# Level 1 of a gated linear attention without a matmul group of its own

## The chip, the cores and the metric

The kernel runs on one core of a Trainium2 chip. The time is that of one execution on the device, in microseconds, from the first to the last instruction with what the device adds around it. Several runs are taken and their median is given.

## The reference

The program is a two-layer block. Each layer mixes three branches (retention with 4 heads, HGRN2 with 8 heads, differential attention with 8 heads) and has a convolutional feed-forward part. There are 16 meta tokens and 256 others, 272 in all, and the width is 1024. The change is in HGRN2 alone, which for one head of 128 features computes, in chunks of 128 tokens,

```python
def step(state, xs):
    qc, kc, vc, lfc = xs
    cb = jnp.cumsum(lfc, axis=1)                  # log of the forget gates, summed
    rel = cb[:, :, None] - cb[:, None, :]
    dec = jnp.where(causal, jnp.exp(jnp.where(causal, rel, 0.0)), 0.0)
    a = jnp.einsum('bqhd,bkhd,bqkhd->bhqk', qc, kc, dec)
    o = jnp.einsum('bhqk,bkhe->bqhe', a, vc) + jnp.einsum('bqhd,bhde->bqhe', qc * jnp.exp(cb), state)
    ...
```

The weight of key k for query q is thus a sum over the features of q times k times the product of the gates of the tokens k+1 to q, and each feature has gates of its own. For k = q there is no gate: the weight is the plain product of q and k.

## The kernel before

**The main stream.** All projections are matmuls of 128x128 weight tiles with 272 (in the second layer partly 258) columns of activations. Each is done three times, with high and low halves of weights and activations (`whi`, `wlo`, `xh`, `xl`; the lines L890 to L892), into tiles named `main`. Weights come by DMA in chunks of eight tiles (`wraw`); ScalarE rounds them to `whi`, and VectorE subtracts to get `wlo`. This stream runs from the beginning to the end, and everything else on TensorE is put between its matmuls.

**The planner.** Every step is recorded as an operation with an engine, a cost and a due time. A list scheduler (`_Plan.order`) then writes an order for every engine, and each engine works its list off in that order. The cost of a group of small matmuls is `0.02 * calls + 0.3`. So a change of one part can move other steps of the same stretch.

**HGRN2 (`hg_heads`).** It is called twice per layer, for the first and the second four heads. The weights within a chunk are built by levels of 64, 32, 16, 8, 4, 2 and 1 tokens: at level s, the tokens are taken in pairs of blocks of s, and the queries of the right block meet the keys of the left one. Queries are multiplied by the gates of their block up to themselves, and keys by the gates behind them; `total` holds the product of gates of each block, and `double` joins two blocks: it multiplies the keys of the left one by the right one's total, and the totals in pairs. The names in the profile are `hq` (queries), `hf` (keys), `he` (gates, the first `total`) and `tot` (later totals).

A group of matmuls for a level is made by `blocks` (L1075): for each head, 32 keys at a time are the stationary side, 128 features deep and 32 columns wide, so that four quarters of the array, each with its 32 columns, write four ranges of 32 partitions of one PSUM bank (`lev`). `quarters` lists the 32 calls of four heads, two chunks and four quarters. Level 4 goes with level 2, and level 16 with level 8: `quads` lists for four blocks of s tokens the queries in six versions (raw, or multiplied ahead), kept in `extra`; a call has 64 columns at level 2 and 48 at level 8. Masked copies (`copy_predicated` with the masks in `lev`) then pick the valid weights into `near`, a tile of 32x32 weights for each quarter, chunk and head. Levels 32 and 64 are made together in a far group of 40 calls (L1075 too), and copied with `near` into `at`, the weights of the four heads.

Before the change, level 1 has a group of its own:

```python
tt(right(q, 1), right(q, 1), right(total, 1), MUL)      # odd queries times their own gate
...
if s == 1:
    wide = pl[:, :256].rearrange("p (g t) -> p g t", g=8)
    quarters(wide, q, lambda hd, c, t: q[:, hd, tokens(c, t)])
    dve.copy_predicated(near, lev[:, 112:144].unsqueeze(1).to_broadcast([P, 8, 32]), wide)
```

Its 32 calls have 32 queries each. From its result the weights of even keys for themselves and for the odd query behind them are taken. The odd queries' own weights come with level 2, from raw odd queries that are part of its list. Afterwards all queries are multiplied by the first gate of their pair, and `double(1, T)` does the keys and totals.

The last 16 of the 272 tokens (the tail) have small matmuls of their own (`pm`, with copies in `kt` and `qt`) for the levels up to 8. For the levels above, the far group has four calls of 16 columns per head with the tail's queries (`late`), multiplied ahead by the totals of one to three blocks of 32 (`last_q`). At the end, the tail's queries are multiplied once more, and `px` takes all keys of the first chunk against the queries of the second chunk and the tail. `hg_outputs` (`ho`, `ht`) multiplies the weights by the values. GpSimd zeroes `at`, `am` and `near` at the start of `hg_heads`. Retention's first steps (`s`, `tw`, `ro`) follow on the second four heads.

Of the kernel before, what the change touches and what calls it, by code (L numbers as in the profile page):

```python
# [14 lines left out]
AF = mybir.ActivationFunctionType  # L15
# [4 lines left out]
P = 128  # L20
# [211 lines left out]
def _constants():  # L232
# [52 lines left out]
    block = [quads(2), quads(8), even(32, 32)]  # L285
    lev[:, :144] = np.tile(np.concatenate(block, axis=1), (4, 1))

# [346 lines left out]
def _trace(ctx, tc, plan, a, depth, probe):  # L634
# [330 lines left out]
    for li in range(depth):  # L965
# [72 lines left out]
        def hg_heads(b):  # L1038
# [30 lines left out]

            def blocks(calls, out, *moving):  # L1070


                def run():
                    for o, keys, x in calls:
                        nc.tensor.matmul(o, keys, x, start=True, stop=True)  # L1075

                plan.add("pe", run, 0.02 * len(calls) + 0.3, [out], [k, *moving])

            def quarters(out, moving, x):

                return blocks([(out[32 * t : 32 * t + 32, 2 * hd + c], k[:, hd, c * P + 32 * t : c * P + 32 * t + 32], x(hd, c, t))
                               for hd in hs for c in range(2) for t in range(4)], out, moving)

# [7 lines left out]


            act.activation(qt2[:, :, 8:], right(q[:, :, tail], 1)[:, :, :, 0], AF.Copy)
            act.activation(quads(2)[:, :, : 2 * P // 8, 12:], q[:, :, : 2 * P].rearrange("p h (n k two) -> p h n k two", k=4, two=2)[:, :, :, :, 1], AF.Copy)
            tt(right(q, 1), right(q, 1), right(total, 1), MUL)
            room, at0 = slot("tot"), 0
            for i, s in reversed(list(enumerate(LEVELS))):
# [4 lines left out]
                if s in (4, 16, 64):  # L1102
                    continue
                pl = bank("lev")
                tokens = lambda c, t: slice(c * P + 32 * t, c * P + 32 * t + 32)
                end = 2 * P if s > 8 else T
                if s == 1:
                    wide = pl[:, :256].rearrange("p (g t) -> p g t", g=8)
                    quarters(wide, q, lambda hd, c, t: q[:, hd, tokens(c, t)])
                    dve.copy_predicated(near, lev[:, 112:144].unsqueeze(1).to_broadcast([P, 8, 32]), wide)  # L1110
                elif s in (2, 8):
                    x = quads(s)
# [10 lines left out]
                    wide = pl[:, : 8 * each * width]  # L1123
                    quarters(wide.rearrange("p (g t) -> p g t", g=8), extra,
                             lambda hd, c, t: x[:, hd, (4 * c + t) * each : (4 * c + t + 1) * each, :].rearrange("p n x -> p (n x)"))
# [9 lines left out]
                    if s == 2:  # L1135
                        dve.copy_predicated(to.rearrange("p g n (k two) -> p g n k two", two=2)[:, :, :, :, 1], mask[:, :, :, 12:], wide[:, :, :, 12:])
                elif s == 32:
                    for t in range(4):
                        here = slice(32 * t, 32 * t + 32)
                        act.activation(at[here, :, : 2 * P].rearrange("p h (c t) -> p h c t", c=2)[:, :, :, here],  # L1140
                                       near[here].rearrange("p (h c) t -> p h c t", c=2), AF.Copy)


                    far_q = extra[:, : 8 * 96].rearrange("p (h n x) -> p h n x", h=4, n=2)
                    last_q = extra[:, 8 * 96 : 8 * 96 + 12 * TAIL].rearrange("p (n h t) -> p n h t", n=3, h=4)
                    qs = q[:, :, : 2 * P].rearrange("p h (n t) -> p h n t", n=2)
                    by = lambda c, m: total[:, :, :8].rearrange("p h (n c) -> p h n c", c=4)[:, :, :, c : c + 1].to_broadcast([P, 4, 2, m])
                    act.activation(far_q[:, :, :, :32], qs[:, :, :, 64:96], AF.Copy)
                    act.activation(far_q[:, :, :, 64:], qs[:, :, :, 96:], AF.Copy)
# [18 lines left out]
                    blocks(calls, far, q, far_q, last_q)  # L1168
                    for n in range(2):
                        for t, cols, x in ((0, slice(0, 96), 3 * n), (1, slice(0, 64), 1 + n), (2, slice(64, 96), 1 + n)):  # L1170
                            to = at[lanes[t], :, n * P + 32 * t + 32 : n * P + P]
                            if t == x:
                                dve.tensor_copy(to, far[lanes[x], :, cols])
                            else:
                                act.activation(to, far[lanes[x], :, cols], AF.Copy)
                    act.activation(at[:, :, tail], far[:, :, 96:], AF.Copy)
# [35 lines left out]
                if s == 1:  # L1212
                    qr = q.rearrange("p h (n two) -> p h n two", two=2)
                    tt(qr, qr, first.to_broadcast([P, 4, n, 2]), MUL)
                elif s in (2, 8):
# [6 lines left out]
                else:  # L1222

                    qr = q[:, :, P + 32 : 2 * P]
                    tt(qr, qr, total[:, :, 4:5].to_broadcast([P, 4, 96]), MUL)
                if s == 2:
                    total = parts
                else:
                    double(s, end, P if s == 32 else None)
# [442 lines left out]
```

## Time and profile before

| | us |
|---|---|
| runs before | 1318.12 median (1317.83 to 1318.2, 3 runs) |
| the profiled execution | 1318.41 |
| its span, first to last instruction | 1316.6 |
| TensorE busy in the span | 1308.1 |
| VectorE busy | 972.7 |
| ScalarE busy | 843.9 |
| GpSimd busy | 83.6 |

The mean granted TensorE clock is 0.999. The profile names TensorE PE, its weight loads PEld, VectorE DVE, ScalarE ACT and GpSimd POOL. Nearly all instructions of the helpers stand under L575, where they are recorded; they are told apart by their tiles. In a row of the timeline, the length of a matmul reaches from its start until its last result, and the next one starts before that: what a matmul costs is read from starts. A matmul of fp32 operands stands in the trace as two records (level 1's 32 calls are `x64`).

### The profile page before, as it was taken

Reading aid. Unit: us, or ns where it says so; the run is one execution under the profiler, and the core shown is the slowest. Engines: PE = TensorE matmul, PEld = TensorE weight load, DVE = VectorE, ACT = ScalarE, POOL = GpSimd, SP = SyncE. Lnnn points to the kernel's source line nnn. Section 1 sums busy time; section 2 is a strip of 40 time slices with the busy share of each in tenths; the row PEclk is TensorE's granted clock in tenths of the full one; section 3 lists DMA queues with packets and bytes.
Section 4 is the critical chain, followed back from the end, with each engine's and each line's share of the span. In section 5 each row is a group of like instructions: output and inputs, shape, how many; then the busy total and the mean of one; then the engine's idle time right before and its main releaser. Section 6 shows DMA issues by size and latency. Waiting matters only on the chain.

```text
span 1316.6 us, 27793 instructions
## 1 busy us (share of the span) xinstructions
PE 1308.1 (99%) x11286; PEld 1284.2 (98%) x11286; DVE 972.7 (74%) x1678; ACT 843.9 (64%) x1426; POOL 83.6 (6%) x161
## 2 busy tenths in 40 slices
PE   9999999999999999999999999999999999999998
PEld 9999999999999999999999999999999999999986
DVE  7685797698586789876564867976885867998753
ACT  6757465747577577776456574657566766777743
POOL 4000000000010020000030000000000100200000
PEclk9999999999999999999999999999999999999999
DMA  7644534453544545555555455354445456465653
GB/s 275 193 153 153 169 123 163 141 161 126 179 145 150 184 160 182 177 178 174 176 177 182 149 166 172 121 175 143 160 130 181 141 161 199 154 205 187 202 181 107
DMA packets 60750, 219.02 MB, mean 166 GB/s; under 512 B 6864, under 2 KB 6992, under 8 KB 60624
## 3 DMA queue, kind: packets, MB, share of 16 engines
q1 hardware_dynamic: 60336, 216.74, 51.5%
q8 instruction: 88, 1.44, 0.5%
q10 hardware_dynamic: 288, 0.52, 0.1%
q14 instruction: 38, 0.31, 0.1%
HBM read 216.19 MB, written 1.05 MB: 165 GB/s over the span
## 4 chain that ended last, share of the span: by engine, by line
PE 97%; DVE 1%; ACT 1%; DMA 0%; issue 0%; SPq 0%; POOL 0%; ACTq 0%
PE main L892 28%; PE main L890 28%; PE main L891 28%; PE fo L1467 2%; PE fo L1469 2%; PE fo L1468 2%; PE ds L1328 1%; PE lev L1075 1%; PE ms L575 1%; PE ho L575 1%; PE ro L575 1%; PE do L575 1%; PE vt L575 1%; PE wt L575 0%; PE s L575 0%; DMA h<-in_h 0%
## 5 line engine op out<-in xcount | busy, mean ns | idle before, releaser
L890 PE MATMUL main<-xh,whi 128*128 128x272 f32 (+1 forms) x2368 | 692.2, 292 | 0.0
L892 PE MATMUL main<-xh,wlo 128*128 128x272 f32 (+1 forms) x2368 | 680.4, 287 | 0.7 <-DVE wlo L575 0.6
L891 PE MATMUL main<-xl,whi 128*128 128x272 f32 (+1 forms) x2368 | 671.6, 284 | 0.0
L575 DVE TENSOR_TENSOR wlo<-wraw,whi 128x1024 fp32r<-128x1024 f32 (+1 forms) x408 | 498.4, 1226 | 223.9 <-ACT whi L575 223.1
L575 ACT ACTIVATE whi<-wraw 128x1024 fp32r<-128x1024 f32 (+1 forms) x408 | 426.9, 1048 | 223.4 <-PE main L891 159.5
L891 PEld LDWEIGHTS main<-xl,whi 128*128 128x128 f32 x2368 | 449.0, 190 | 0.6
L890 PEld LDWEIGHTS main<-xh,whi 128*128 128x128 f32 x2368 | 445.6, 188 | 1.5
L892 PEld LDWEIGHTS main<-xh,wlo 128*128 128x128 f32 x2368 | 444.5, 188 | 1.6 <-DVE wlo L575 1.6
L575 DVE SCALAR_TENSOR_TENSOR two_b<-u,small,two_b 128x256 f32<-128x256 f32 (+2 forms) x176 | 82.1, 508 | 0.9 <-ACT two_b L575 0.9
L575 POOL TENSOR_TENSOR y<-h,rstd 128x272 f32<-128x272 f32 x32 | 36.2, 1167 | 314.6 <-ACT rstd L575 314.6
L575 ACT ACTIVATE two_b<-u,small 128x272 f32<-128x272 f32 (+1 forms) x88 | 50.0, 598 | 4.3 <-DVE u L575 2.1
L892 PE MATMUL main<-ghi,wlo 128*128 128x272 f32 x176 | 51.0, 290 | 0.0
L890 PE MATMUL main<-ghi,whi 128*128 128x272 f32 x176 | 50.9, 289 | 0.0
L891 PE MATMUL main<-glo,whi 128*128 128x272 f32 x176 | 50.2, 285 | 0.0
L575 ACT ACTIVATE u<-main 128x544 f32<-128x544 f32 (+1 forms) x36 | 22.2, 615 | 35.1 <-PE main L892 35.1
L890 PE MATMUL main<-b1hi,whi 128*128 128x272 f32 (+1 forms) x128 | 37.9, 296 | 0.0
L890 PE MATMUL main<-b0hi,whi 128*128 128x272 f32 (+1 forms) x128 | 37.8, 295 | 0.0
L575 POOL COPY tails<-vsrc 128x32 f32<-128x32 f32 x32 | 10.3, 335 | 418.3 <-ACT vsrc L575 365.9
L892 PE MATMUL main<-yhi,wlo 128*128 128x272 f32 (+1 forms) x128 | 36.7, 286 | 0.0
L892 PE MATMUL main<-b2hi,wlo 128*128 128x272 f32 (+1 forms) x128 | 36.7, 286 | 0.0
L892 PE MATMUL main<-b1hi,wlo 128*128 128x272 f32 (+1 forms) x128 | 36.6, 286 | 0.0
L892 PE MATMUL main<-b0hi,wlo 128*128 128x272 f32 (+1 forms) x128 | 36.6, 286 | 0.0
(246 smaller groups left out, 1958.5 us busy)
## 6 DMA issues: line engine op xcount, KB each, us to landing
wraw<-in_w SPq DMA_DIRECT2D x402, 512.0 KB, 3.6
h<-in_h SPq DMA_DIRECT2D x4, 272.0 KB, 5.7
dec<-in_dec SPq DMA_DIRECT2D x2, 544.0 KB, 5.0
wraw<-in_w SPq DMA_DIRECT2D x4, 256.0 KB, 5.4
const<-in_const SPq DMA_DIRECT2D x1, 937.0 KB, 5.7
gain<-in_gl SPq DMA_DIRECT2D x1, 512.0 KB, 4.9
out<-y ACTq DMA_DIRECT2D x2, 256.0 KB, 2.8
out<-y SPq DMA_DIRECT2D x2, 256.0 KB, 2.7
```

The lines of the kernel that those rows point to most:

```text
L575: self.plan.add(self.name, lambda: f(*args, **kw), cost, outs, ins, args[2] if method == "activation" else None)
L890: nc.tensor.matmul(o, wh, hi, start=first, stop=False)
L891: nc.tensor.matmul(o, wh, lo, start=False, stop=False)
L892: nc.tensor.matmul(o, wl, hi, start=False, stop=last)
L1075: nc.tensor.matmul(o, keys, x, start=True, stop=True)
L1328: nc.tensor.matmul(ss[m][:, at : at + nk], q[half, hd, q0 : q0 + P], k[half, hd, :nk], start=True, stop=True)
L1467: nc.tensor.matmul(o, gh, wh, start=False, stop=False)
L1468: nc.tensor.matmul(o, gl, wh, start=False, stop=False)
L1469: nc.tensor.matmul(o, gh, wl, start=False, stop=end)
```

## The change

Level 1 has no group any more.

- The raw odd queries that go in level 2's list now meet, through a mask of both tokens of a pair, the even key as well as their own. The even key has by then been multiplied by the odd token's gate, as the keys are doubled first.
- The weights of even tokens for themselves are sums over the features of query times key. A product of both (`own`, 4 x 128 columns, kept in `at` before that tile is zeroed) is made at the start; four calls with 32 columns of ones as the stationary side sum it over the partitions, at the end of level 8's group, into the rest of the same PSUM bank. One more masked copy puts them into `near`. The zeroing of `at` comes after it.
- In the far group, the tail's queries are appended to the lists of chunk 1's queries: 28 calls in place of 40, of 112, 96, 80, 64, 48, 32 and 16 columns per head. The tail's queries are multiplied along with the others.

```diff
-                out.append(key == 8 * n + 1 + 2 * np.arange(4)[None, :])
+                out.append(key // 2 == 4 * n + np.arange(4)[None, :])
...
+    ones_1 = fixed([P, 32], "ones_1")
+    pool.memset(ones_1, 1.0)
...
-            pool.memset(at, 0.0)
...
+            def quarters(out, moving, too, x):
+                calls = [(out[32 * t : 32 * t + 32, 2 * hd + c], k[:, hd, c * P + 32 * t : c * P + 32 * t + 32], x(hd, c, t))
+                         for hd in hs for c in range(2) for t in range(4)]
+                if not too:
+                    return blocks(calls, [out], moving)
+                evens, own = too
+                own_8 = own.rearrange("p h (c t) -> p h c t", c=2)
+                for t in range(4):
+                    calls.append((evens[32 * t : 32 * t + 32], ones_1, own_8[:, :, :, 16 * t : 16 * t + 16]))
+                return blocks(calls, [out, evens], moving, own)
...
+            own = at[:, :, :P]
+            every = lambda t: t[:, :, : 2 * P].rearrange("p h (n two) -> p h n two", two=2)[:, :, :, 0]
+            tt(own, every(k), every(q), MUL)
...
-            tt(right(q, 1), right(q, 1), right(total, 1), MUL)
...
-                if s == 1:
-                    wide = pl[:, :256].rearrange("p (g t) -> p g t", g=8)
-                    quarters(wide, q, lambda hd, c, t: q[:, hd, tokens(c, t)])
-                    dve.copy_predicated(near, lev[:, 112:144].unsqueeze(1).to_broadcast([P, 8, 32]), wide)
...
+                    else:
+                        dve.copy_predicated(near.rearrange("p g (n two) -> p g n two", two=2)[:, :, :, 0],
+                                            lev[:, 112:P].unsqueeze(1).to_broadcast([P, 8, 16]), evens)
+                        pool.memset(at, 0.0)
...
-                    late = [q[:, :, tail]]
-                    for n in range(3):
-                        tt(last_q[:, n], late[-1], total[:, :, 7 - n : 8 - n].to_broadcast([P, 4, TAIL]), MUL)
-                        late.append(last_q[:, n])
+                    act.activation(raw_q, q[:, :, tail], AF.Copy)
+                    tt(far_q[:, :, 1, 112:], q[:, :, tail], late(3), MUL)
+                    tt(far_q[:, :, 1, 64:80], far_q[:, :, 1, 112:], late(2), MUL)
+                    tt(q[:, :, tail], far_q[:, :, 1, 64:80], late(1), MUL)
...
-                        calls += [(far[lanes[3 * n], hd, :96], keys(n * P), q[:, hd, n * P + 32 : n * P + P]) for n in range(2)]
-                        calls += [(far[lanes[1 + n], hd, :64], keys(n * P + 32), far_q[:, hd, n, :64]) for n in range(2)]
-                        calls += [(far[lanes[1 + n], hd, 64:96], keys(n * P + 64), far_q[:, hd, n, 64:]) for n in range(2)]
-                        calls += [(far[lanes[t], hd, 96:], keys(P + 32 * t), late[3 - t][:, hd, :]) for t in range(4)]
+                        calls += [(far[lanes[0], hd, :], keys(P), q[:, hd, P + 32 : T]),
+                                  (far[lanes[3], hd, :96], keys(0), q[:, hd, 32:P]),
+                                  (far[lanes[1], hd, 32:], keys(P + 32), far_q[:, hd, 1, :80]),
+                                  (far[lanes[2], hd, :64], keys(32), far_q[:, hd, 0, :64]),
+                                  (far[lanes[2], hd, 64:], keys(P + 64), far_q[:, hd, 1, 80:]),
+                                  (far[lanes[1], hd, :32], keys(64), far_q[:, hd, 0, 80:112]),
+                                  (far[lanes[3], hd, 96:], keys(P + 96), raw_q[:, hd, :])]
...
+                    for t in range(4):
+                        to = at[lanes[t], :, P + 32 * t + 32 : T]
+                        dve.tensor_copy(to, far[lanes[t], :, 32 * t :])
+                        if t < 3:
+                            to = at[lanes[t], :, 32 * t + 32 : P]
+                            act.activation(to, far[lanes[3 - t], :, : 96 - 32 * t], AF.Copy)
...
+                        tt(right(qt1, 1), right(qt1, 1), right(total[:, :, tail], 1), MUL)
...
-                    tt(qr, qr, first.to_broadcast([P, 4, n, 2]), MUL)
+                    tt(qr[:, :, :, 0:1], qr[:, :, :, 0:1], first, MUL)
+                    double(1, T)
+                    tt(qr[:, :, :, 1], qr[:, :, :, 1], total, MUL)
...
-                    qr = q[:, :, P + 32 : 2 * P]
-                    tt(qr, qr, total[:, :, 4:5].to_broadcast([P, 4, 96]), MUL)
+                    qr = q[:, :, P + 32 :]
+                    tt(qr, qr, total[:, :, 4:5].to_broadcast([P, 4, 96 + TAIL]), MUL)
...
-            tt(q[:, :, tail], q[:, :, tail], total[:, :, 1:2].to_broadcast([P, 4, TAIL]), MUL)
```

More of the change, by code (lines that the diff above doesn't have):

```diff
@@ L284, in _constants @@
     lev = np.zeros((P, 3 * 64 + 192), f)
-    block = [quads(2), quads(8), even(32, 32)]
-    lev[:, :144] = np.tile(np.concatenate(block, axis=1), (4, 1))
+    block = [quads(2), quads(8), np.arange(32)[:, None] == 2 * np.arange(16)[None, :]]
+    lev[:, :128] = np.tile(np.concatenate(block, axis=1), (4, 1))
     inner = [even(TAIL, 16), level(2, TAIL, 8), odd(TAIL, 8), level(4, TAIL, 8), level(8, TAIL, 8)]
@@ L1068, in right, with blocks @@
                 return halves(t, s, t.shape[2])[:, :, :, 1, :]
-            def blocks(calls, out, *moving):
+            def blocks(calls, outs, *moving):
                 def run():
@@ L1075, in run @@
                         nc.tensor.matmul(o, keys, x, start=True, stop=True)
[L1077 to L1082, printed above, removed]
+                plan.add("pe", run, 0.02 * len(calls) + 0.3, outs, [k, *moving])
+            def quarters(out, moving, too, x):
[8 more added lines that the diff above has]
+                return blocks(calls, [out, evens], moving, own)
             extra = gate_tile("extra").rearrange("p k t -> p (k t)")
@@ L1103, in hg_heads @@
                     continue
-                pl = bank("lev")
-                tokens = lambda c, t: slice(c * P + 32 * t, c * P + 32 * t + 32)
                 end = 2 * P if s > 8 else T
-                if s == 1:
-                    wide = pl[:, :256].rearrange("p (g t) -> p g t", g=8)
-                    quarters(wide, q, lambda hd, c, t: q[:, hd, tokens(c, t)])
-                    dve.copy_predicated(near, lev[:, 112:144].unsqueeze(1).to_broadcast([P, 8, 32]), wide)
-                elif s in (2, 8):
+                if s > 1:
+                    pl = bank("lev")
+                if s in (2, 8):
                     x = quads(s)
@@ L1123, in hg_heads @@
                     wide = pl[:, : 8 * each * width]
-                    quarters(wide.rearrange("p (g t) -> p g t", g=8), extra,
+                    evens = pl[:, 3 * P : 4 * P].rearrange("p (g t) -> p g t", g=8)
+                    quarters(wide.rearrange("p (g t) -> p g t", g=8), extra, s == 8 and (evens, own),
                              lambda hd, c, t: x[:, hd, (4 * c + t) * each : (4 * c + t + 1) * each, :].rearrange("p n x -> p (n x)"))
@@ L1163, in hg_heads @@
                         keys = lambda t: k[:, hd, t : t + 32]
-                        calls += [(far[lanes[3 * n], hd, :96], keys(n * P), q[:, hd, n * P + 32 : n * P + P]) for n in range(2)]
-                        calls += [(far[lanes[1 + n], hd, :64], keys(n * P + 32), far_q[:, hd, n, :64]) for n in range(2)]
-                        calls += [(far[lanes[1 + n], hd, 64:96], keys(n * P + 64), far_q[:, hd, n, 64:]) for n in range(2)]
-                        calls += [(far[lanes[t], hd, 96:], keys(P + 32 * t), late[3 - t][:, hd, :]) for t in range(4)]
[L1168 to L1176, printed above, removed]
+                        calls += [(far[lanes[0], hd, :], keys(P), q[:, hd, P + 32 : T]),
[5 more added lines that the diff above has]
+                                  (far[lanes[3], hd, 96:], keys(P + 96), raw_q[:, hd, :])]
+                    blocks(calls, [far], q, far_q, raw_q)
+                    for t in range(4):
[4 more added lines that the diff above has]
+                            act.activation(to, far[lanes[3 - t], :, : 96 - 32 * t], AF.Copy)
                 def tails(i, s):
```

9 lines of the change are left out of this document (5 added, 4 removed).

## The prediction

> **What bounds the kernel now.** I read the page first, for the engine that is never idle.
>
> ```profile
> span 1316.6 us, 27793 instructions
> ## 1 busy us (share of the span) xinstructions
> PE 1308.1 (99%) x11286; PEld 1284.2 (98%) x11286; DVE 972.7 (74%) x1678; ACT 843.9 (64%) x1426; POOL 83.6 (6%) x161
> ```
>
> TensorE (PE) is busy in 1308.1 of 1316.6 us, so time comes out of this kernel in two ways only: PE gets less to do, or one of its few waits goes. The second view is the list of what PE itself waited for in all of the span; after one wait at the start, before any projection, it has three rows (us in total, times, longest):
>
> ```profile
> PE main L892 <- DVE wlo L575: 0.6, 3, 0.2
> PE wt L575 <- POOL dt L575: 0.2, 1, 0.2
> PE px L575 <- DVE hq L575: 0.2, 1, 0.2
> ```
>
> Only the last row lies where the change is. The third view is PE's timeline around the level-1 group of the first four heads in layer 0; each row has start, length, engine, line and operation.
>
> ```profile
> 76.81 0.29 PE L891 MATMUL main<-xl,whi 128*128 128x272 f32 x1
> ...
> 78.80 0.29 PE L892 MATMUL main<-xh,wlo 128*128 128x272 f32 x1
> 79.02 0.76 PE L1075 MATMUL lev<-hq,hf 128*32 128x32 f32 x64
> 79.71 0.39 PE L890 MATMUL main<-xh,whi 128*128 128x272 f32 x1
> 79.94 0.29 PE L891 MATMUL main<-xl,whi 128*128 128x272 f32 x1
> ```
>
> The projections (`main`) start one after another: from 76.81 to 78.80 there are 16 steps, so one takes 0.124 us. The lengths of 0.29 overlap and are not costs; starts are. The group stands in the same queue, and nothing hides it.
>
> **The level-1 group goes: 4 x -0.89 us.** Between the last `main` before it and the second one after it lie 79.94 - 78.80 = 1.14 us, where two steps alone would take 0.25. The group costs 0.89, of which 0.69 (79.02 to 79.71) is its own stretch and 0.20 is spent at its two edges, where PE turns from 128-wide to 32-wide matmuls and back. There is one such group per four heads and layer, so four: **-3.56 us**. The edges agree with the Trainium skill ("TensorEngine Tiling (Array Packing)", Key Properties), which says that a change of the tiling mode drains TensorE; that is why a whole group is worth more than its columns.
>
> **The sums by ones come: 4 x +0.22.** The level-8 group gets four more calls with 128 moving columns, one for each 32-column quarter of the array. The nearest row is another fp32 matmul with 128 columns, over the full width:
>
> ```profile
> 84.35 0.29 PE L892 MATMUL main<-xh,wlo 128*128 128x272 f32 x1
> 84.48 0.38 PE L575 MATMUL pm<-qt,kt 128*128 128x128 f32 x2
> 84.61 0.37 PE L890 MATMUL main<-xh,whi 128*128 128x272 f32 x1
> 84.82 0.28 PE L891 MATMUL main<-xl,whi 128*128 128x272 f32 x1
> ```
>
> 84.82 - 84.35 = 0.47, less two steps: 0.22 us. If the four run side by side in their quarters, all cost 0.22; in series 0.87. The level-1 group decides: 32 calls of 32 columns would take 32 x 0.22/4 = 1.76 us in series, and took 0.69. So the quarters do overlap, and I take 0.22: **+0.87**; the upper end, +3.5, is kept for the range. No edge is added, since the group is there anyway.
>
> **The far group has 28 calls in place of 40: 4 x -0.08.**
>
> ```profile
> 99.99 0.28 PE L1075 MATMUL lev<-hq,hf 128*32 128x96 f32 x2
> ...
> 101.06 0.39 PE L890 MATMUL main<-xh,whi 128*128 128x272 f32 x1
> ```
>
> It takes 1.07 us. Both versions move 448 columns per head, 112 in each quarter, so the columns cost the same; only short calls become fewer (16-wide ones 16 to 4, 32-wide 8 to 4). A short call is worth at most what one of level 1 cost, 0.69/32 = 0.022 us, and 12 fewer at most 0.26; the least is nothing. As most short calls ran beside longer ones in other quarters I take a third, 0.08: **-0.3**.
>
> PE's own work thus falls by 3.56 + 0.3 - 0.87 = **3.0 us**.
>
> **The wait of px: -0.7.** `px` needs the last products on q and k, which DVE makes. Undisturbed, in the first four heads:
>
> ```profile
> 103.66 0.29 PE L892 MATMUL main<-xh,wlo 128*128 128x272 f32 x1
> 103.78 0.65 PE L575 MATMUL px<-hq,hf 128*128 128x144 f32 x4
> 104.18 0.38 PE L890 MATMUL main<-xh,whi 128*128 128x272 f32 x1
> ```
>
> and in the second four of layer 0 and of layer 1:
>
> ```profile
> 199.75 0.29 PE L892 MATMUL main<-xh,wlo 128*128 128x272 f32 x1
> 200.23 0.73 PE L575 MATMUL px<-hq,hf 128*128 128x144 f32 x4 [0.19 <-DVE hq L575]
> 200.70 0.38 PE L890 MATMUL main<-xh,whi 128*128 128x272 f32 x1
> ```
>
> ```profile
> 857.82 0.28 PE L892 MATMUL main<-xh,wlo 128*128 128x258 f32 x1
> 858.13 0.73 PE L575 MATMUL px<-hq,hf 128*128 128x144 f32 x4
> 858.60 0.37 PE L890 MATMUL main<-xh,whi 128*128 128x258 f32 x1
> ```
>
> From `main` to `main`: 0.52 undisturbed, 0.95 and 0.78 here. PE loses 0.43 and 0.26 = 0.69 us, more than the waits list tells, because the end of the matmul before is counted as busy. DVE is the late one, and it is full in this stretch (the windows view; the columns are PE, PEld, DVE, ACT, POOL):
>
> ```profile
> 171.00:201.00 30.00, 29.81 (x479) 28.81 (x478) 28.87 (x61) 19.63 (x42) 2.70 (x6) 1.00 0.41 134
> ```
>
> So DVE's sum decides. Its rows in this stretch, by form, with the mean in ns behind the comma:
>
> ```profile
> L575 DVE TENSOR_TENSOR hq<-hq,he 128x1088 f32<-128x1088 f32 x1 | 1.3, 1283 | 0.0
> ...
> L575 DVE TENSOR_TENSOR hq<-hq,he 128x544 f32<-128x544 f32 x1 | 0.7, 707 | 0.0
> ...
> L575 DVE COPY_PREDICATED near<-masks,lev 128x256 f32<-128x256 uint8 x1 | 0.5, 455 | 0.2 <-PE lev L1075 0.2
> ...
> L575 DVE COPY at<-lev 32x384 f32<-32x384 f32 x1 | 0.5, 546 | 0.0
> ```
>
> The two products give 0.13 us + 1.06 ns per element; the rest is an estimate from that line. Per four heads there go: both products above (1.99), the level-1 copy (0.46 and 0.2 of waiting for PE), four products of 64 (0.80), one of 384 (0.54), three copies of 384, 256 and 128 (about 1.26): 5.25 with the wait. There come: key times query (512 elements, 0.67), two products of 544 (1.41), one of 32 (0.16), the copy of the even tokens (128, 0.33), three products of 64 (0.60), one of 448 (0.60), four copies of 448, 320, 192 and 64 (about 1.7): 5.5. DVE pays about +0.2 us. But the zeroing of `at` on GpSimd moves away from the stretch's beginning, and there stands:
>
> ```profile
> 170.54 0.42 DVE L575 TENSOR_SCALAR he<-he,keep,floor 128x272 f32<-128x272 f32 x1
> 170.87 0.36 DVE L575 TENSOR_SCALAR hf<-hf,keep 128x272 f32<-128x272 f32 x1
> 171.14 1.26 DVE L575 TENSOR_SCALAR he<-he,keep,floor 128x272 f32<-128x272 f32 x1
> ```
>
> ```profile
> 171.24 1.00 POOL L575 MEMSET at<- 128x1088 f32 x1
> ```
>
> The same instruction takes 1.26 beside the memset and 0.42 without: 0.84 us of DVE. At its new place, after the level-8 matmuls, DVE does products and copies with masks; whether it holds those up no row shows (0 to 0.84). Taking 0, as no `TENSOR_SCALAR` stands there, DVE arrives 0.6 us earlier. Besides, the built order of the changed kernel puts `px` of these heads 14 `main` triples later (476 instead of 462 in layer 0), 14 x 0.37 = 5.2 us. What is late next is retention's first step, whose small product is now queued right behind `px`; I expect at most 0.2 us there. The wait goes: **-0.7**.
>
> In other places DVE's extra 0.2 is hidden: PE waited for DVE's weights (`wlo`) 0.6 us in all the span. If that cover is gone, 0.2 a group, +0.8. ScalarE loses the copy of the tail's far columns and gains a copy of the raw tail, one each of 64 columns: nothing. GpSimd's memset now waits for the level-8 matmuls, with the copy of value tails behind it in its queue; GpSimd is 6% busy, so nothing. The list of DMAs is the same.
>
> **Sum.** -3.0 - 0.7 = **-3.7 us**. The profiled execution took 1318.41 us (span 1316.6 and 1.8 around it), 0.3 above the median of 1318.12. 1318.41 - 3.7 = 1314.7 for an execution like that; against the median **1314.4 us**, or -0.28%. About 0.2% (2.6 us) is what a measurement of this kernel can tell from no change, so "faster" begins below 1315.5.
>
> **Rivals.** *(a) The waits move rather than go.* Only PE's work counts: -3.0 -> 1315.1; with a hidden cost of 0.4 or more come back at `px` or `ro`, 1315.5 to 1316. For it: DVE is still full in the stretch and the memset could block it at the new place (0.84). Against: the 5.2 us. Chance 0.22, half of it on either side of the bound.
>
> *(b) The four sums run in series, in part or wholly.* An fp32 call comes as two records in the trace (x64 for 32 calls). If the second record of one quarter has to start ahead of the next quarter's first, five halves of 0.11 us follow each other, 0.55 a group: -3.7 + 4 x 0.33 = -2.4 -> 1315.7. Wholly in series they cost 0.87, 0.65 more than I take: -3.7 + 2.6 = -1.1 -> 1317.0. Neither can be told from no change. For it: they are the longest calls of the group, and each must begin behind its quarter's last 48-wide call. Against: level 1's 0.022 us a call, where one such call alone would take 0.055. Chance 0.10. The Trainium skill ("TensorE: Matmul & The Clock Gate", Step-by-step: what each phase is for) says that matmuls stay in program order and only weight loads are pulled ahead, which is the first of the two cases; the level-1 row doesn't agree with it for calls in different quarters.
>
> *(c) Slower.* The new order packs retention's first steps behind the late `px`: what was spread over some 20 triples is pressed together by the 5.2 us that `px` moved. If DVE and ScalarE can't follow, PE stands in both layers; it becomes slower by 0.2% once that passes 3.7 + 2.6 = 6.3 us in all, 3.2 a layer, and if all of the shift came back as standing, 2 x 5.2 - 3.7 = +6.7 -> 1324.8. Against: the products in question are small and DVE has 0.6 us more room. Chance 0.05.
>
> *The change doesn't do what it says:* the built program has 128 of the 32-wide calls fewer, 16 sums more and 48 far calls fewer; so no chance to that.
>
> **Numbers.** Forecast 0.63; (a) 0.22, (b) 0.10, (c) 0.05. Faster: 0.63 + 0.11 = 0.74 less 0.02 for a far group that gains nothing together with a small wait, 0.72. Same: 0.11 + 0.10 + 0.02 = 0.23; slower 0.05. The likeliest case alone spans 1313.7 to 1315.2; with (a) above, and below the 0.3 us by which the profiled execution and the median differ, the range is 1313.4 to 1316.2.
>
> **What would show it.** Right: no 32-wide group at level 1; the level-8 group's stretch, first `lev` to next `main`, longer by about 0.22 us; far groups near 1.0; `px` in the second heads with 0.52 from `main` to `main`; `TENSOR_SCALAR he` at 0.42 throughout. Wrong: a level-8 group longer by 0.5 us or more (b), waits of PE for DVE at `px`, `ro` or `main` of over 0.5 us (a, c), masked copies twice as long beside the memset.

## The result, and the profile after

| | before | after |
|---|---|---|
| median, us | 1318.0 (1317.7 to 1318.59, 9 runs) | 1314.39 (1313.97 to 1314.69, 9 runs) |
| ratio to before | | 0.9972, 95% interval 0.9962 to 0.9982 |
| profiled execution, us (span) | 1318.41 (1316.6) | 1314.0 (1312.2) |

The changed kernel is 3.6 us faster; the forecast was 1314.4. The number came out, but not by all of its terms: most of one (the wait of `px`) comes back as other waits, and a place that the forecast put at nothing happens to pay for it, so the closeness is partly luck. First the page of after:

```profile
span 1312.2 us, 27174 instructions
## 1 busy us (share of the span) xinstructions
PE 1304.9 (99%) x10966; PEld 1281.9 (98%) x10966; DVE 972.1 (74%) x1686; ACT 842.6 (64%) x1426; POOL 84.2 (6%) x162
```

PE is as full as before, with 320 records less. In the list of PE's waits the row of `px` is gone, and of the three waits for `wlo` one is left (the run ctl below, which changes nothing in the stream, has two; so that number scatters):

```profile
PE wt L576 <- POOL dt L576: 0.2, 1, 0.2
PE main L895 <- DVE wlo L576: 0.2, 1, 0.2
```

The level-8 group of the second heads of layer 0, where `pm` follows in both kernels, before:

```profile
188.90 0.29 PE L892 MATMUL main<-xh,wlo 128*128 128x272 f32 x1
189.12 0.89 PE L1075 MATMUL lev<-extra,hf 128*32 128x48 f32 x64
189.94 0.43 PE L575 MATMUL pm<-qt,kt 128*128 128x64 f32 x2
...
190.39 0.28 PE L891 MATMUL main<-xl,whi 128*128 128x272 f32 x1
```

and after:

```profile
187.67 0.29 PE L895 MATMUL main<-xh,wlo 128*128 128x272 f32 x1
187.88 0.89 PE L1077 MATMUL lev<-extra,hf 128*32 128x48 f32 x64
188.59 0.40 PE L1077 MATMUL lev<-at,ones 128*32 128x128 f32 x8
188.92 0.43 PE L576 MATMUL pm<-qt,kt 128*128 128x64 f32 x2
...
189.37 0.28 PE L894 MATMUL main<-xl,whi 128*128 128x272 f32 x1
```

From the last `main` to the second one behind: 1.49 us before, 1.70 after. The eight records of the four sums cost 0.21. The far group of the first heads, whose first row before stood at 99.99 with `main` at 101.06:

```profile
96.22 0.28 PE L1077 MATMUL lev<-hq,hf 128*32 128x112 f32 x2
96.23 0.33 PE L1077 MATMUL lev<-extra,hf 128*32 128x80 f32 x4
...
97.24 0.39 PE L893 MATMUL main<-xh,whi 128*128 128x272 f32 x1
```

1.02 us in place of 1.07. And `px` of the second heads, both pairs:

```profile
203.08 0.29 PE L895 MATMUL main<-xh,wlo 128*128 128x272 f32 x1
203.21 0.65 PE L576 MATMUL px<-hq,hf 128*128 128x144 f32 x4
203.60 0.38 PE L893 MATMUL main<-xh,whi 128*128 128x272 f32 x1
...
204.31 0.28 PE L895 MATMUL main<-xh,wlo 128*128 128x272 f32 x1
204.56 0.61 PE L576 MATMUL px<-hq,hf 128*128 128x144 f32 x3
```

The first pair runs undisturbed (0.52 from `main` to `main`). The second should start one step (0.124) behind 204.31 and starts 0.25 behind: a wait that the waits list does not show, since the matmul before it is still counted as busy. VectorE's rows tell what it hangs on:

```profile
202.60 0.23 DVE L576 COPY at<-lev 32x64 f32<-32x64 f32 x1
202.86 1.23 DVE L576 TENSOR_TENSOR wlo<-wraw,whi 128x1024 fp32r<-128x1024 f32 x1
204.12 0.29 DVE L576 TENSOR_TENSOR tw<-s,const 128x128 f32<-128x128 f32 x1
```

`tw<-s`, which reads retention's scores out of their PSUM bank, ends at 204.41, and `px` starts 0.15 later. In the changed program the banks of this kind, two in turn, are taken by far group, `s`, `px`, `px`: the first `px` needs the far group's bank, the second that of `s`. The waits in the program say the same, in both layers: the first `px` there waits for VectorE's last copy out of the far group's bank (`at<-lev`), the second for `tw<-s`, and `px` reads neither `at` nor `tw`.

**Where the time went.** I compare the start of the n-th `main` in both traces; a difference between two such numbers tells what a stretch gained or lost, whatever the start did.

| stretch | after less before, us | PE work of the change | rest |
|---|---|---|---|
| layer 0, first heads | -0.65 | -0.76 | +0.11 |
| layer 0, second heads | -0.93 | -0.73 | -0.43 of `px` gone, +0.23 new |
| layer 1, first heads | -0.72 | -0.77 | +0.05 |
| layer 1, second heads | -0.78 | -0.73 | -0.26 of `px` gone, +0.21 new |
| all of it, from the first heads to the last `main` | -3.07 | -2.99 | about nothing |
| behind the last matmul's start | -0.49 | | |

PE work is -0.89 + 0.215, less what the far group saves: 0.083 and 0.098 in the first heads, and 0.053 in the second, where other matmuls stand beside it and it is taken from the run far below. The first heads of layer 0 have a new wait, too: their `px`, seven projection triples earlier than before, now starts late for its own products (`hq` ends at 99.46, `px` starts at 99.61). The last row can be seen in the page: from the start of VectorE's last instruction to the end of the span there are 5.05 us before and 4.55 after.

```profile
1311.55 0.75 DVE L575 SCALAR_TENSOR_TENSOR y<-fo,dm,gain 128x512 f32<-128x512 f32 x1 [1.47 <-ACT dm L575]
```

```profile
1307.65 0.75 DVE L576 SCALAR_TENSOR_TENSOR y<-fo,dm,gain 128x512 f32<-128x512 f32 x1 [1.47 <-ACT dm L576]
```

-3.07 - 0.49 = -3.56, against 3.6 between the medians. The profiled pair differs by 0.8 us more, ahead of the first 100 projections; that is scatter from one execution to the next: the run memlate below starts 0.6 us earlier than before's profile, too, and has before's median.

### The profile page after: what moved, and what is told of

Same layout as the page of the kernel before. It is cut to its first block, busy times and chain, and to the rows that moved or that the text cites. A ratio compares the mean times of both kernels' runs of the same rounds, so it can differ in the third digit from the quotient of the medians.

```text
span 1312.2 us, 27174 instructions
## 1 busy us (share of the span) xinstructions
PE 1304.9 (99%) x10966; PEld 1281.9 (98%) x10966; DVE 972.1 (74%) x1686; ACT 842.6 (64%) x1426; POOL 84.2 (6%) x162
## 4 chain that ended last, share of the span: by engine, by line
PE 98%; DVE 1%; DMA 0%; ACT 0%; issue 0%; SPq 0%; POOL 0%; DVEq 0%
PE main L895 29%; PE main L893 29%; PE main L894 28%; PE fo L1485 2%; PE fo L1487 2%; PE fo L1486 2%; PE ds L1346 1%; PE lev L1077 1%; PE ms L576 1%; PE ro L576 1%; PE ho L576 1%; PE do L576 1%; PE vt L576 1%; PE s L576 0%; PE wt L576 0%; DMA h<-in_h 0%
## 5 line engine op out<-in xcount | busy, mean ns | idle before, releaser
L893 PE MATMUL main<-yhi,whi 128*128 128x272 f32 (+1 forms) x128 | 36.5, 285 | 0.0
```

The costliest lines, as they stand in the source:

```text
L893: nc.tensor.matmul(o, wh, hi, start=first, stop=False)
```

## The experiments

Medians are device us; the ratio is to the kernel before, measured beside it.

**The new tile of ones alone.** The kernel before with

```
+    ones_1 = fixed([P, 32], "ones_1")
+    pool.memset(ones_1, 1.0)
```

> The kernel before with only the tile of ones and its memset (128x32, GpSimd) added at the start; no instruction of any engine moves. In the two profiles at hand the changed kernel's first projections are already 0.8 us ahead at 20 us, long before HGRN2 begins, while its four HGRN2 stretches give 0.64, 0.93, 0.72 and 0.78 us, 3.07 together. Theory A (all of the gain comes from HGRN2, the start is scatter between executions): ratio 1.000, 1318.0 within 0.3 us. Rival B (the extra memset or what goes with it shortens the start): about 0.5 us faster, 1317.5, and the profile's main stream ahead of before by 0.5 to 0.8 us at 20 us.

1317.98, ratio 1.0 (0.9991 to 1.0009). Nothing; the trace starts as before's does.

**Level 1's group alone.** The kernel before without the 32 calls and the masked copy of level 1, so the weights of neighbouring tokens and the tokens' own are left out; the group keeps its place and its cost in the order.

```
-                    quarters(wide, q, lambda hd, c, t: q[:, hd, tokens(c, t)])
-                    dve.copy_predicated(near, lev[:, 112:144].unsqueeze(1).to_broadcast([P, 8, 32]), wide)
+                    plan.add("pe", lambda: None, 0.02 * 32 + 0.3, [wide], [k, q])
```

> The kernel before without the 32 calls of level 1 and without the masked copy that reads them; the weights of even keys for themselves and for the next query are left out of the result. The planner is given the same cost in their place. Theory A (the group costs its own stretch and both edges, 0.89 us): 4 x 0.89 = 3.56 us less; and px, which the planner sets after retention's first step here (8 main triples later in layer 0), waits less, 0 to 0.7: 1313.7 to 1314.5. Rival B (part of the group was hidden, only its stretch of 0.69 counts): 2.8 us less, 1315.2 or, with px's waits, 1314.5 to 1315.2. The timelines tell: from the last main before to the second main after, the 1.14 us become 0.25.

1314.19, ratio 0.9972 (0.996 to 0.9983). Each group's gap falls from 1.14 to 0.25 us, -0.88 in each of the four places. The first term stands. Both `px` of the second heads, with the masked copy (0.46) off VectorE and eight triples later in the order, start without a wait.

**The far group alone.** The kernel before with the changed far group, its queries and its copies (the hunks from `far_q` to the copies, and the last product on the tail's queries taken into the one of level 32):

```
-            tt(q[:, :, tail], q[:, :, tail], total[:, :, 1:2].to_broadcast([P, 4, TAIL]), MUL)
```

> The kernel before with only the far group as in the changed one: 28 calls, the tail's queries in chunk 1's lists, and the products and copies that go with it. Theory A (only short calls are saved): the stretch from the first far call to the next main falls from 1.07 to about 1.0 us, four times 0.08 is 0.3 us less; px stays where it was in the second heads and waits about as long (0.43 and 0.26), since its last product on the tail is gone (0.2) and the copies are longer: 1317.4 to 1318.0. Rival B (the wait of px hung on that last product): the waits of px go too, 0.7 more, 1317.0.

1317.09, ratio 0.9993 (0.9984 to 1.0002): the time alone is not told from no change, the trace tells more. The far group of layer 0's first heads takes 1.22 in place of 1.30 (the whole gap, less two steps), -0.083; the others, in order, gain 0.053, 0.096 and 0.053, 0.285 in all. And `px` of the second heads:

```profile
198.75 0.29 PE L892 MATMUL main<-xh,wlo 128*128 128x272 f32 x1
198.88 0.65 PE L575 MATMUL px<-hq,hf 128*128 128x144 f32 x4
199.27 0.38 PE L890 MATMUL main<-xh,whi 128*128 128x272 f32 x1
```

0.52: no wait, at the same place in the order (projection triple 461; 462 before) and with the memset where it was. In the kernel before VectorE's last product ahead of `px` was that on the tail's queries:

```profile
199.07 0.88 DVE L575 TENSOR_TENSOR hf<-hf,tot 128x256 f32<-128x256 f32 x2
199.87 0.22 DVE L575 TENSOR_TENSOR hq<-hq,tot 128x64 f32<-128x64 f32 x1
```

It ended at 200.09 and `px` started at 200.23. It is that product that `px` waited for. But it takes only 0.13 us of VectorE's queue, and the wait was 0.43. In the run far the planner also sets one of the `wlo` products and a copy out of the far group's bank, both ahead of the products on q and k before, behind them (in layer 1 a copy alone):

```profile
196.57 0.87 DVE L575 TENSOR_TENSOR hf<-hf,tot 128x256 f32<-128x256 f32 x2
197.35 1.22 DVE L575 TENSOR_TENSOR wlo<-wraw,whi 128x1024 fp32r<-128x1024 f32 x1
```

So the products end at 197.44, 1.44 us ahead of `px` (0.50 in layer 1). Neither the memset's new place nor a later `px` is needed for the wait to go; which share the product has, and which the new order, was not run apart.

**The memset later, in the kernel before.**

```
-            pool.memset(at, 0.0)
...
+                    if s == 8:
+                        pool.memset(at, 0.0)
```

> The kernel before with only the zeroing of at moved from the start of the HGRN2 part to behind level 8's masked copies. Theory A (DVE was 0.84 us late in the second heads because of the memset): TENSOR_SCALAR he takes 0.42 in place of 1.26 us at the beginning of both stretches, and px's waits of 0.43 and 0.26 go: 0.7 us less, 1317.3. The planner also puts px behind retention's first step, 10 main triples later in layer 0. Rival B (at the new place the memset holds up masked copies or products as long): DVE gains nothing; any gain then is from the new place of px alone, and the masked copies into near last up to 1 us longer than 0.38, 0.23 and 0.30.

1317.9, ratio 0.9999 (0.999 to 1.0008). The edit did not do what it was made for: the order of the work is made from due times, and the memset, which had nothing to wait for, went to its old place:

```profile
170.67 1.01 POOL L575 MEMSET at<- 128x1088 f32 x1
```

`he` takes 1.26 beside it as before. What the edit did move is `px`, ten triples later: the first one then starts without a wait (0.49 over the steps), with the memset still early. But in layer 0 the second one stands, at 205.17 behind a `main` at 204.82: it takes the bank of `s`, and `tw<-s` ends at 205.11. Over the second heads 0.36 us come back in layer 0 and 0.29 in layer 1. So a later place, one of the two reasons that the prediction gave for the gain at `px`, takes the wait for the products away and gains nothing.

**The sums by ones twice.** The changed kernel with each of the four calls made twice, one more in each 32-column quarter:

```
-                for t in range(4):
+                for t in (0, 1, 2, 3, 0, 1, 2, 3):
                     calls.append((evens[32 * t : 32 * t + 32], ones_1, own_8[:, :, :, 16 * t : 16 * t + 16]))
```

> The changed kernel with each of the four sums by ones called twice (one more call in each 32-column quarter, same result, same order of the work). Theory A (calls in different quarters run side by side, a quarter is held for 0.214 us by one call): the level-8 group gets 0.21 us longer, four times, +0.86: 1315.25 us against 1314.39 of the changed kernel. Rival B (the sums follow each other, and what the changed kernel paid for four was hidden in the end of the 48-wide calls): four more cost 4 x 0.22 = 0.87 a group, +3.5: 1317.9 us.

**Four more sums in one quarter.** The same with `(0, 1, 2, 3, 0, 0, 0, 0)`.

> The changed kernel with four more sums by ones, all of them in the first 32-column quarter (same result, same order of the work). Theory A (a quarter is a queue of its own: 0.214 us for each call in the same quarter): the level-8 group gets 4 x 0.214 = 0.86 us longer, +3.4 in all: 1317.8 us, back at the kernel before. Rival B (the array takes calls as they come, whatever the quarter): the same as one more call in each quarter, +0.86: 1315.25 us.

1314.8, ratio 0.9978 (0.9968 to 0.9987), and 1317.52, ratio 0.9997 (0.9988 to 1.0006). The sums' rows in the first heads of layer 0, spread and in one quarter:

```profile
91.18 0.62 PE L1077 MATMUL lev<-at,ones 128*32 128x128 f32 x16
```

```profile
90.91 1.25 PE L1077 MATMUL lev<-at,ones 128*32 128x128 f32 x16
```

The gap of the level-8 group with `pm`, less two steps, is 1.455 in the changed kernel, 1.675 with four more calls spread and 2.31 with four more in one quarter: +0.22 and +0.855, four times as much. Each quarter works off its calls by itself here, at 0.214 us per call. By the starts of `main` both cost 0.4 less than 4 x 0.22 and 4 x 0.855 say (0.5 and 3.0 in place of 0.9 and 3.4): PE then comes later to `px`, and the waits there go. In ones_row, where no wait is left to be seen, the group of `px`, `ro` and `s` costs 1.417 and 1.391 us, in the changed kernel 1.612 and 1.555, and the first heads' `px` 0.10 less. So the changed kernel still loses 0.10 + 0.195 + 0.164 = 0.46 us in waits there.

**The memset early, in the changed kernel.**

```
-            own = at[:, :, :P]
+            own = slot("own")[:, : 4 * P].rearrange("p (h t) -> p h t", h=4)
...
+            pool.memset(at, 0.0)
             pool.memset(am, 0.0)
...
-                        pool.memset(at, 0.0)
```

> The changed kernel with the memset of at back at its early place (the products key times query get a tile of their own). Theory A (the wait of px hung on the last product on the tail's queries, which the change takes away, not on the memset): TENSOR_SCALAR he takes 1.26 us again, but px of the second heads still starts without a wait, and px and ro together lose at most 0.1 us more than in the changed kernel: 1314.4, at most 1314.6 us. Rival B (the prediction's reason: the memset's 0.84 us of VectorE at the beginning of the stretch decide): px or ro of the second heads wait 0.3 to 0.8 us more in each layer: 1315.0 to 1316.0 us.

1315.2, ratio 0.9978 (0.9969 to 0.9987). `he` takes 1.25 again, and `px` of the second heads waits, 0.24 and 0.23 us. VectorE, then PE, in layer 0:

```profile
203.49 0.23 DVE L576 COPY at<-lev 32x64 f32<-32x64 f32 x1
```

```profile
203.58 0.29 PE L895 MATMUL main<-xh,wlo 128*128 128x272 f32 x1
203.87 0.73 PE L576 MATMUL px<-hq,hf 128*128 128x144 f32 x4
```

The last copy out of the far group's bank ends at 203.72, 0.9 us later than in the changed kernel, while PE is 0.5 later, and `px` follows by 0.15. The products that `px` reads had been ready for four microseconds. So rival B is right that the memset's 0.84 us count in the changed kernel, but through the bank. By stretches the loss is 0.38 in layer 0 and about nothing in layer 1, where the order differs (`s` further ahead, no `ro` behind `px`), 0.28 in all. The medians differ by 0.8. The remaining half microsecond lies behind the last matmul: 6.74 us from its start to the end, as before (6.78), where the changed kernel has 6.29.

**The copies off VectorE and GpSimd.** The changed kernel with

```
-                        dve.tensor_copy(to, far[lanes[t], :, 32 * t :])
+                        act.activation(to, far[lanes[t], :, 32 * t :], AF.Copy)
...
-                    pool.tensor_copy(st[f"dt{b}"][:, g, hd, :], w[:, c : c + TAIL])
+                    act.activation(st[f"dt{b}"][:, g, hd, :], w[:, c : c + TAIL], AF.Copy)
```

> The changed kernel with the four copies of the far group that VectorE made (at, chunk 1) on ScalarE, and the copies of the tail's attention weights (dt) on ScalarE in place of GpSimd. Theory A (what is left of the waits at px and ro, 0.10 + 0.19 + 0.16, hangs on VectorE's queue, which gets 1.7 us shorter per four heads; the two waits of 0.38 at wt hang on GpSimd's copy of dt): both go, -0.45 - 0.76, at most 1.2 us: 1313.2 to 1313.9 us. Rival B (ScalarE, which makes the weights' rounded halves in between, becomes late in VectorE's place): PE waits for ScalarE at main or px instead, no gain: 1314.4 us or up to 1 us more.

1314.44, ratio 0.9972 (0.9961 to 0.9982): no gain, as rival B had it, but theory A's waits did go. The second heads gained 0.19 and 0.15 us, `wt` 0.62 (in layer 1 only), and the first heads of layer 1 lost 0.8 to 0.9:

```profile
757.72 2.47 ACT L576 ACTIVATE at<-lev 32x448 f32<-32x448 f32 x6
```

```profile
760.33 0.45 PE L576 MATMUL ho<-at,vt 128*128 128x114 f32 x2 [0.45 <-ACT at L576]
```

In the first heads `ho`, which needs all of `at`, is due beside `px`, and ScalarE's queue of copies is late there.

**Six idle instructions on GpSimd.** In the changed kernel, ones_two, ones_row and atactdt the end behind the last matmul's start is 6.3 us; in all the others so far 6.65 to 6.8. The trace's records, waits and drains counted, show GpSimd standing 0.29 us longer there ahead of its 197th instruction (0.36 in place of 0.07), in kernels with 201 or 202 of them; a drain next to it then takes 0.14 to 0.22 us in place of 0.08. With 207 (the changed kernel) it has passed that instruction beside other work, with 175 (atactdt) it does not come to it. The kernel before with

```
+    pad_1 = fixed([P, 1], "pad_1")
+    for _ in range(6):
+        pool.memset(pad_1, 1.0)
```

> The kernel before with six memsets of one column more on GpSimd, at the start, and nothing else; GpSimd then executes 207 instructions, as in the changed kernel, instead of 201. Theory A (0.45 us of the changed kernel's gain lie behind the last matmul, where GpSimd stands 0.29 us ahead of its 197th instruction and then drains in 0.21 in place of 0.08 us; with six instructions more ahead of it the 197th is passed earlier, beside other work): from the last matmul's start to the end 6.3 us instead of 6.78, main's starts unchanged, 1317.55 us against 1318.0. Rival B (the end's difference comes with something else in the change): 6.7 to 6.8 us, 1318.0 us.

**The same in memearly.**

> The kernel of the run memearly with the same six memsets on GpSimd. Theory A (of the 0.8 us by which memearly is behind the changed kernel, 0.45 are GpSimd's end and 0.3 the waits at px and ro): 1314.75 us, the end 6.3 us behind the last matmul's start, px of the second heads as in memearly (0.24 us of wait). Rival B (all 0.8 are the memset's, in the waits): 1315.2 us.

1315.83, ratio 0.9985 (0.9977 to 0.9994), and 1313.14, ratio 0.9963 (0.9949 to 0.9976): 2.0 and 2.1 us faster than without, where theory A had 0.45. The ends are 6.34 and 6.35 us, so theory A holds for what it speaks of: in all fourteen traces the short end goes with 175 or 207 instructions and the long one with 201 or 202 (the new tile came with the six here; it was not run by itself with 201). The other 1.7 us come from a place that neither theory had: the last 1000 projections of layer 1, from about 1129 us, step by 118.1 ns in place of 119.7. No instruction of PE was changed:

```profile
PE 1305.9 (99%) x11286; PEld 1281.8 (97%) x11286; DVE 972.3 (74%) x1678; ACT 843.0 (64%) x1426; POOL 84.3 (6%) x167
```

1305.9 busy in place of 1308.1, with the same 11286 records. The six instructions or the tile, which moves all later tiles in SBUF by 32 bytes, do that; the tile of ones in ctl, which moves the same tiles by 128 bytes, does not. The last two runs tell them apart.

**A better version.** The changed kernel with ScalarE's copies only where they gained:

```
-                        dve.tensor_copy(to, far[lanes[t], :, 32 * t :])
+                        if b:
+                            act.activation(to, far[lanes[t], :, 32 * t :], AF.Copy)
+                        else:
+                            dve.tensor_copy(to, far[lanes[t], :, 32 * t :])
...
-                    pool.tensor_copy(st[f"dt{b}"][:, g, hd, :], w[:, c : c + TAIL])
+                    act.activation(st[f"dt{b}"][:, g, hd, :], w[:, c : c + TAIL], AF.Copy)
```

> The changed kernel with the second heads' four copies of the far group (at, chunk 1) on ScalarE, the first heads' left on VectorE, and the copies of the attention weights of the tail (dt) on ScalarE. Theory A (waits are local: the second heads' px and ro gain 0.18 and 0.15 us as in the run atactdt, wt's wait goes, 0.62 us in that run, and the 0.8 us that atactdt lost at ho in the first heads of layer 1 stay away): -0.95 us, 1313.45 us. Rival B (what ScalarE takes over makes it late elsewhere, as it did at ho in that run): 1314.0 to 1314.5 us.

1313.31, ratio 0.9966 (0.9953 to 0.9978), 1.1 us below the changed kernel, as theory A had it. The first heads stay as they were, the second gain 0.19 and 0.15, `wt` 0.62.

**The same with one more tile.**

```
+    fixed([P, 1], "pad_1")
```

> The kernel of the run best with one tile of one column more at the start of the fixed tiles, which moves every later tile by 32 bytes; no instruction is added. In poolpad and memearlypad, which have this tile and six memsets, the last 1000 projections of layer 1 (from about 1138 us on) started every 118.1 ns in place of 119.7, 1.7 us in all. Theory A (the place of the tiles does it): the same here, 1313.3 - 1.7 = 1311.6 us, and GpSimd's end as in best (6.3 us). Rival B (GpSimd's six instructions do it): 119.7 ns and 1313.3 us.

1311.73, ratio 0.9955 (0.9941 to 0.9968): theory A, the place of the tiles. The windows of both, best first (PE's records are in the first brackets):

```profile
1060.00:1120.00 60.00, 60.00 (x504) 60.00 (x502) 43.10 (x52) 37.53 (x46) 0.41 (x2) 1.00 0.56 182
1140.00:1200.00 60.00, 60.00 (x503) 60.00 (x503) 54.36 (x96) 45.42 (x77) 0.00 (x0) 1.00 0.61 193
```

```profile
1060.00:1120.00 60.00, 60.00 (x504) 60.00 (x503) 43.00 (x51) 37.62 (x46) 0.42 (x2) 1.00 0.56 183
1140.00:1200.00 60.00, 60.00 (x510) 60.00 (x510) 55.09 (x98) 46.16 (x77) 0.00 (x0) 1.00 0.60 194
```

PE is busy throughout in both, at a granted clock of 1.00, and still puts 510 matmuls where it put 503; in the window from 1060 there is no difference. This version is 6.2 us faster than the kernel before and 2.7 faster than the changed one.

## Why the prediction came out, point by point

- **Level 1's group, -3.56.** Right: -0.88 in each place when it alone is taken out, and no 32-wide group in the trace of after.
- **The sums by ones, +0.87.** Right: +0.214 a group, and the reason is shown: one more call in every quarter costs 0.22, four in one quarter 0.855. Rival (b) is out. The Trainium skill ("TensorE: Matmul & The Clock Gate", Step-by-step: what each phase is for) says that matmuls stay in program order. The trace does not agree for calls in different quarters: the far group of after begins with calls of 112, 96, 80 and 64 columns, and their second records start at 96.342, 96.335, 96.329 and 96.322, the last call first.
- **The far group, -0.3.** Right, -0.285 in all (0.053 to 0.098 a group); the third that I took of the short calls' worth was an estimate that happened to fit.
- **The wait of `px`, -0.7.** This is the step that failed, in its net size and in half of its reason. The wait for VectorE's products went in the second heads (0.43 and 0.26), and "14 x 0.37 = 5.2 us" of later place is enough for that, as memlate shows with the memset where it was; but the run far shows that other changes of VectorE's order do it, too, so "DVE arrives 0.6 us earlier" because of the memset is not needed. With the later place `px` got another thing to wait for, the banks that the far group's copies and `tw<-s` give back. I had looked at the data that `px` reads, not at the bank that it writes. "At most 0.2" for what is late next held in each place (0.195 and 0.164), but I did not take it off the 0.7, nor did I look at the first heads (0.10): 0.46 us are seen as waits, and by stretches about 0.6 came back of 0.69. Rival (a), -3.0 with waits that move, is what PE's stream shows: -3.07.
- **"GpSimd is 6% busy, so nothing".** Wrong: 0.45 to 0.49 us at the end hang on the number of GpSimd's instructions. This term, put at nothing, made up for the one that failed, which is luck. Without it the time would have been 1314.8 to 1314.9, near rival (a)'s 1315.1.
- **The memset at its new place, 0.** Right: it ran from 189.08 to 190.09 us, and the three masked copies beside it took 0.38, 0.23 and 0.30 us; before, without it, they took 0.37, 0.23 and 0.30. The fourth copy of the row below is the new one of the even tokens; it starts behind the memset and takes 0.45 (forecast 0.33). `he` in layer 0 and those copies, after:

```profile
169.66 0.42 DVE L576 TENSOR_SCALAR he<-he,keep,floor 128x272 f32<-128x272 f32 x1
...
189.23 1.46 DVE L576 COPY_PREDICATED near<-masks,lev 128x192 f32<-128x192 uint8 x4
```

and the copies before:

```profile
190.07 0.97 DVE L575 COPY_PREDICATED near<-masks,lev 128x192 f32<-128x192 uint8 x3
```

- **Rival (c), slower.** No sign: no wait of PE for VectorE or ScalarE in the second heads exceeds 0.2 us.

Three things stay open. That `px` waits for banks rests on the waits in the program, on its following the banks' last readers by 0.15 us in the changed kernel and in memearly, and on the wait's going where these readers come earlier; a third bank was not tried. Why GpSimd stands ahead of its 197th instruction is not known. And why a shift of 32 bytes makes 1000 projections faster is not known: other stages with the same tiles kept their 119.7 ns in the shifted kernels.

## What to carry to other kernels

Ask of a matmul not only what it reads but whose bank it writes: when its inputs come earlier, the last reader of that bank, queued on an engine that is full, is late next. A gain on PE ahead of such a place is partly paid back as a wait there, and extra PE work ahead of it is partly free, so price an edit by the stretch, over equal numbers of instructions, and not by the waits list. When a median moves by a few tenths of a per cent, look at the ends of the trace and at the step of the unchanged instructions too: here the number of instructions on an idle engine and a 32-byte shift were worth 0.45 and 1.7 us, as much as what one designs.

## What the runs showed of the hardware that I had not expected

- An idle engine's number of instructions counts at the end: 201 or 202 instructions on GpSimd cost 0.35 to 0.49 us there, against 207 or 175.
- The same fp32 matmuls with 258 columns step by 119.7 or 118.1 ns, at a granted clock of 1.00; moving all tiles by 32 bytes switched the last 1000 of them from one to the other in three kernels.
- GpSimd and VectorE hinder each other by the kind of instruction: `TENSOR_SCALAR` took 1.26 us beside a memset in place of 0.42, while masked copies (0.38, 0.23, 0.30) and the products for `wlo` (1.21) took no longer beside it; and GpSimd's copy of 16 columns, 0.20 us by itself, took 1.13 beside VectorE's products for `wlo` (the `dt` that `wt` waits for).
